# A hybrid Hyena/retention step: Hyena product in three pieces, residual chain rebuilt around adaLN work, two weight halves ahead in the opening

## The chip, the core and the metric

The kernel runs on one core of a Trainium2 chip. The metric is device time in microseconds (us) of one launch. The core has a matrix engine (TensorE, PE in the rows), three elementwise engines (VectorE = DVE, ScalarE = ACT, GpSimd = POOL), and SyncE (SP), which issues most of the transfers from memory. Each engine works through its own list of instructions in the order in which it was written; engines wait for one another through semaphores. A list that is held at its first instruction holds all that stands behind it.

## What is computed

One layer on two groups of 128 tokens of width 2048 (g = 0: context tokens, g = 1: latent tokens). Cut to what matters here:

```python
mod = silu(c) @ w_ada + b_ada              # 6 x 2048: shift, scale, gate for mixer and FFN (adaLN)
h   = rmsnorm(x, g_pre_m) * (1 + scale_m) + shift_m
proj = h @ w_in                            # Hyena v, x1, x2; retention q, k, v, g; two gates
z    = x1 * fftconv(v, kf[0], bias[0])     # convolution of 128 tokens by a Fourier product
y_hy = x2 * fftconv(z, kf[1], bias[1])
y_ret = retention(q, k, v, state) * silu(g)
merged = g_hy * (y_hy @ w_br_hy) + g_ret * (y_ret @ w_br_ret)
x = x + gate_m * rmsnorm(merged @ w_out, g_post_m)       # first residual
h2 = rmsnorm(x, g_pre_f) * (1 + scale_f) + shift_f
a, b = split(dwconv3(h2 @ ffn_w_up))
x = x + gate_f * rmsnorm((gelu(a) * b) @ ffn_w_down, g_post_f)
```

## The kernel before

**Products.** A weight matrix is read in *halves* of 256 x 512 numbers (512 KB). A half arrives as `raw`; ScalarE casts it to the upper part `wh` (L225) and VectorE subtracts to get the lower part `wl` (L226). The activations stand in two parts too (`hTh`, `hTl` and the like). TensorE then makes three products for each 128 rows and each group: wh with the upper part (L292), wl with the upper part (L293), wh with the lower part (L294); 12 matmuls for a half, 6 where the two groups are made apart.

**Order.** The program is written out by a planner, item by item (`run_items`). An item is the matmuls of one half or some adaLN matmuls (`ada`, L575). Behind each item `feed` writes splits until `st["L"]` halves are split ahead of their use, and transfers until `st["R"]` raws are outstanding; `depth(L, R)` sets both. `defer(us, f)` writes f once the planned matmul time has gone on by that many us, and small pieces of side work (`push`, `piece(cost, f)`) are written as a time budget allows; `drain` writes all that is left of them at once. What the planner wrote is the fixed order of each engine's list.

**Opening (about 25 to 285 us).** The adaLN vector for the mixer is made in six blocks (`mod_block`), each two or four columns of 128. For each: `ada` matmuls, a copy `adap` (L579), transposes `pcol` (L622), `colsum` and `colA` on VectorE, the affine step on `xnT`, then `hTh` on ScalarE (L678) and `hTl` on VectorE (L680). Eight projections over that block follow, with the next block's adaLN woven in. Halves of `w_in` are counted from 0 in this text; blocks after the first begin at halves 8, 16, 24, 32 and 48. Depth is `depth(3, 10)` (L719). Beside it runs the filter network of the convolution: `p` (L462), a sine chain `arg` on VectorE (L444 to L449), `h1T` on ScalarE (L450).

**Hyena (about 290 to 520 us).** As side work, `conv_fwd` (L794) makes two Fourier products `pu`, `pa`, six VectorE operations for the complex product `y` (L803 to L805), then `yh` and `yl` (L807, L808). The adaLN columns for the FFN (`ada_todo`, L709) run among the projections; their columns are turned (`to_cols`) 2.0 us of planned time after the last `ada` matmul.

**First residual (about 840 to 910 us).** `w_out` is multiplied in four column chunks. For the last ten halves (two of the third chunk, all eight of the fourth) the two groups stand apart, all of g = 0 before g = 1, so that the residual of g = 0 is made while TensorE does g = 1. `out_evac` takes squares (`jk`, L1271) and the gate product (`gm`, L1272); `chain_a` adds to x (`xr`, L1226) and squares (L1228); `chain_b` (L1232ff) ends in `diag` (L376), a diagonal matrix of 1/rms; `h2_block` turns 4 x 128 columns with it (`pt`, L1249), applies scale and shift (`h2v`, L1255, L1258) and splits (`h2Th` L1260, `h2Tl` L1261). The up-projection of the FFN begins with g = 0 of ten halves (`up_first`, L1388), counted 240 to 249 here, then their g = 1; `w_out`'s last chunk is 232 to 239.

Of the kernel before, what the change touches and what calls it, by code (L numbers as in the profile page):

```python
# [100 lines left out]
def hybrid_step(ctx: ExitStack, tc: tile.TileContext, ins, y_p, y_s, st_out):  # L101
# [692 lines left out]
    def conv_fwd(o, g, hf, src):  # L794
        def f():
            cs = slice(hf * W, hf * W + W)
# [43 lines left out]
    def hyena():  # L840
# [5 lines left out]
        F = lambda o, i: piece(4.8, conv_fwd(o, *gh[i], io[o][0]), True)  # L846
        I = lambda o, i: piece(0.6, conv_inv(o, *gh[i], io[o][1]), True)

        def fin(o):
            def f():  # L850
# [8 lines left out]
             load("x1", 1), S(0, 0), mul("x1", 0, 0), F(0, 0), S(0, 1), mul("x1", 0, 1), load("x2", 0), F(0, 1),  # L859
             I(0, 0), mul("x1", 1, 0), S(0, 2), mul("x1", 1, 1), load("x2", 1), F(0, 2), I(0, 1), S(0, 3),  # L860
             mul("x2", 0, 0), F(0, 3), I(0, 2), mul("x2", 0, 1), S(1, 0), mul("x2", 1, 0), I(0, 3), fin(0), F(1, 0),
             S(1, 1), mul("x2", 1, 1), F(1, 1), I(1, 0), S(1, 2), F(1, 2), I(1, 1), S(1, 3), F(1, 3), I(1, 2),
# [358 lines left out]
    def chain_a(g):  # L1221

        r = neg2_rstd(ssm[:, g, NBLK - 1:NBLK], mbase[g])
        ssx = small([P, 3], "ssx")
# [4 lines left out]
        xbase[g] = ssx

    def chain_b(g):
        ssx, b0, b1 = xbase.pop(g), small([P, 1], "b0"), small([P, 1], "b1")
        V.tensor_tensor(out=b0, in0=ssx[:, 0:1], in1=ssx[:, 1:2], op=ALU.add)
        V.tensor_scalar(out=b1, in0=b0, scalar1=1.0 / D, scalar2=RMS_EPS, op0=ALU.mult, op1=ALU.add)
        dg2[g] = diag_of(neg2_rstd(ssx[:, 2:3], b1))
        for h in range(2):
# [4 lines left out]

    def h2_block(g, j):
        def f():
# [3 lines left out]
            pt = aux((P, 4, P), "pt")  # L1247
            for kk in range(4):
                PE.matmul(pt[:, kk, :], lhsT=xr[g, j // 2][:, (j % 2) * W + kk * P:(j % 2) * W + (kk + 1) * P],  # L1249
                          rhs=dg2[g], start=True, stop=True)  # L1250
            val = s2("h2v").rearrange("p (a t) -> p a t", a=4)
            for kk in range(4):
                sc, sh = colA[:, 3, 4 * j + kk, g:g + 1], colA[:, 2, 4 * j + kk, g:g + 1]
# [259 lines left out]
```

## Time and profile before

| | us |
|---|---|
| median of three runs | 1639.85 (1639.69 to 1643.77) |
| the profiled execution | 1639.68 |
| its span in the trace | 1637.9 |
| TensorE busy | 1588.7, 97% of the span |
| TensorE weight loads busy | 1249.3, 76% |
| VectorE busy | 1191.9, 73% |
| ScalarE busy | 733.4, 45% |
| mean granted TensorE clock | 0.988 of full speed |

The span is 1.8 us shorter than the execution's time; what lies around it is nothing that the kernel orders. TensorE is idle 49 us in all, and more than half of that lies in the first 25 us and the last 10. So a change can take away only the few waits between, and the matmuls that run at half clock behind some of them; every wait that it adds shows in the time at once. The clock has two levels here, 1.0 (2.4 GHz) and 0.50 (1.2 GHz).

### The profile page before, as it was taken

To read this page: it belongs to the slowest core of one execution; us is meant where nothing else is said; L and a number is where in the kernel's file an instruction comes from. 1 tells how busy PE (TensorE), PEld (TensorE's weight loads), DVE (VectorE), ACT (ScalarE), POOL (GpSimd) and SP (SyncE) were. 2 spreads that over 40 slices of the span, in tenths; PEclk is the share of its full clock that TensorE was granted. 3 is DMA by queue.
4 is the path that set the end of the run, shared out by engine and by line. 5 is a ranking of instruction groups with operands and counts; after the bars stand their busy time and mean duration, and the time that the engine had idled before them with its cause. 6 is when DMAs were issued, how large, how long until landed. Compare 5 with 4: busy or idle time off the path is not lost.

```text
span 1637.9 us, 20339 instructions
## 1 busy us (share of the span) xinstructions
PE 1588.7 (97%) x7449; PEld 1249.3 (76%) x7449; DVE 1191.9 (73%) x1659; ACT 733.4 (45%) x946; POOL 69.0 (4%) x129
## 2 busy tenths in 40 slices
PE   5899999998999999999998999999999999999997
PEld 3566668776677887778887888888888888888886
DVE  2687866977775797678997655777778767778655
ACT  4523333243335346344545555455444355555532
POOL 0000012220001200000000000000000000000000
PEclk9899999999999999999999999999999999999999
DMA  9969898896676888898766765766678866766671
GB/s 331 336 187 326 280 311 267 259 343 201 206 245 220 296 267 298 306 335 279 266 201 219 227 173 179 215 200 200 211 249 266 298 184 190 216 206 203 207 239 52
DMA packets 208477, 396.88 MB, mean 242 GB/s; under 512 B 13221, under 2 KB 29920, under 8 KB 208377
## 3 DMA queue, kind: packets, MB, share of 16 engines
q1 hardware_dynamic: 201336, 373.88, 70.4%
q0 software_dynamic: 6800, 21.62, 4.2%
q8 instruction: 58, 0.95, 0.2%
q14 instruction: 43, 0.34, 0.1%
q10 hardware_dynamic: 240, 0.08, 0.0%
HBM read 384.03 MB, written 6.30 MB: 238 GB/s over the span
## 4 chain that ended last, share of the span: by engine, by line
PE 89%; DVE 4%; DMA 3%; issue 1%; SPq 1%; ACT 1%; DVEq 0%; ACTq 0%
PE acc L292 27%; PE acc L293 26%; PE acc L294 26%; PE ada L575 4%; DMA raw<-in_w_in_dram 2%; SPq L210 1%; PE put L1357 1%; DVE wl L226 1%; PE ph L484 1%; DMA raw<-in_ffn_w_up_dram 0%; ACT wh L225 0%; DMA vr<-in_norm_pre_mix_dram 0%; PE pt L403 0%; DVE h2v L1255 0%; PE pe L479 0%
## 5 line engine op out<-in xcount | busy, mean ns | idle before, releaser
L226 DVE TENSOR_TENSOR wl<-raw,wh 128x1024 fp32r<-128x1024 f32 x504 | 597.9, 1220 | 214.0 <-ACT wh L225 209.7
L225 ACT CAST wh<-raw 128x1024 fp32r<-128x1024 f32 x504 | 508.2, 1048 | 210.0 <-DMA raw<-in_w_in_dram 46.4
L292 PE MATMUL acc<-wh,hTh 128*128 128x512 f32 x704 | 285.0, 405 | 3.2 <-ACT wh L225 3.2
L292 PE MATMUL acc<-wh,h2Th 128*128 128x512 f32 x704 | 278.8, 396 | 1.7 <-ACT h2Th L1260 1.7
L293 PE MATMUL acc<-wl,hTh 128*128 128x512 f32 x704 | 277.4, 394 | 1.4 <-DVE wl L226 1.2
L294 PE MATMUL acc<-wh,hTl 128*128 128x512 f32 x704 | 276.6, 393 | 0.0
L294 PE MATMUL acc<-wh,h2Tl 128*128 128x512 f32 x704 | 275.3, 391 | 0.0
L293 PE MATMUL acc<-wl,h2Th 128*128 128x512 f32 x704 | 274.5, 390 | 0.0
L292 PEld LDWEIGHTS acc<-wh,hTh 128*128 128x128 f32 x704 | 133.7, 190 | 54.9 <-issue 19.5
L604 DVE SCALAR_TENSOR_TENSOR adac<-raw,cT,adac 128x512 f32<-128x512 f32 x240 | 164.6, 745 | 0.0
L293 PEld LDWEIGHTS acc<-wl,hTh 128*128 128x128 f32 x704 | 133.9, 190 | 29.7 <-DVE wl L226 3.0
L294 PEld LDWEIGHTS acc<-wh,hTl 128*128 128x128 f32 x704 | 133.6, 190 | 29.0
L294 PEld LDWEIGHTS acc<-wh,h2Tl 128*128 128x128 f32 x704 | 132.5, 188 | 28.8 <-DVE h2Tl L1261 0.4
L292 PEld LDWEIGHTS acc<-wh,h2Th 128*128 128x128 f32 x704 | 132.6, 188 | 28.4 <-ACT h2Th L1260 2.2
L293 PEld LDWEIGHTS acc<-wl,h2Th 128*128 128x128 f32 x704 | 132.8, 189 | 26.3
L292 PE MATMUL acc<-wh,actTh 128*128 128x512 f32 x352 | 137.3, 390 | 0.0
L294 PE MATMUL acc<-wh,actTl 128*128 128x512 f32 x352 | 137.1, 389 | 0.0
L293 PE MATMUL acc<-wl,actTh 128*128 128x512 f32 x352 | 137.0, 389 | 0.0
L1362 ACT ACTIVATE uv<-put,fcw 128x256 f32<-128x256 f32 x88 | 41.6, 474 | 86.4 <-DVE uv L1365 64.4
L1343 ACT COPY u<-acc 128x512 f32<-128x512 f32 x44 | 25.7, 587 | 119.7 <-PE acc L294 118.0
L294 PEld LDWEIGHTS acc<-wh,actTl 128*128 128x128 f32 x352 | 66.1, 188 | 13.9
L293 PEld LDWEIGHTS acc<-wl,actTh 128*128 128x128 f32 x352 | 66.1, 188 | 13.7
(311 smaller groups left out, 1595.9 us busy)
## 6 DMA issues: line engine op xcount, KB each, us to landing
raw<-in_w_ada_dram SPq DMA_DIRECT2D x192, 512.0 KB
raw<-in_w_in_dram SPq DMA_DIRECT2D x176, 512.0 KB
raw<-in_ffn_w_up_dram SPq DMA_DIRECT2D x176, 512.0 KB
raw<-in_ffn_w_down_dram SPq DMA_DIRECT2D x88, 512.0 KB
raw<-in_w_out_dram SPq DMA_DIRECT2D x32, 512.0 KB
raw<-in_w_br_hy_dram SPq DMA_DIRECT2D x16, 512.0 KB
raw<-in_w_br_ret_dram SPq DMA_DIRECT2D x16, 512.0 KB
shw<-in_hy_short_w_dram POOLq DMA_DIRECT2D x18, 256.0 KB, 8.3
```

The costliest lines, as they stand in the source:

```text
L210: SP.dma_start(out=h.raw.rearrange("p a n -> p (a n)").rearrange("p (a n) -> p a n", a=per), in_=h.src)
L225: A.copy(h.hi, h.raw)
L226: V.tensor_tensor(out=h.lo, in0=h.raw, in1=h.hi.bitcast(F32), op=ALU.subtract)
L292: PE.matmul(self.ps[g], lhsT=h, rhs=wh, start=first, stop=False)
L293: PE.matmul(self.ps[g], lhsT=h, rhs=wl, start=False, stop=False)
L294: PE.matmul(self.ps[g], lhsT=l, rhs=wh, start=False, stop=last)
L484: PE.matmul(ph, lhsT=h2fT, rhs=fl["w3", o, d][:, hf * W:hf * W + W], start=True, stop=True)
L575: PE.matmul(z["ps"][32 * t:32 * t + 32, :nt * P], lhsT=cT[:, kb + kk, 2 - 2 * i:34 - 2 * i], rhs=w[:, kk, :], start=i == 0 and kb + kk < 4 ...
L604: V.scalar_tensor_tensor(out=t, in0=w, scalar=c, in1=t if kt else bias, op0=ALU.mult, op1=ALU.add)
L1343: A.copy(u[:, g, :], ch.ps[g])
L1357: PE.transpose(pt[:, a, g, :], u[:, g, kk * P:(kk + 1) * P], ident)
L1362: A.activation(o, i, AF.Copy, scale=fcw[:, 1, col:col + 1])
```

## The change

It has three parts, and some bookkeeping.

**Opening.** `depth(3, 10)` becomes `depth(2, 8)` from the first block on until the projections behind the blocks: two halves split ahead instead of three, eight raws outstanding instead of ten.

**Hyena.** `conv_fwd` becomes three pieces of side work: the Fourier matmuls with the first half of the complex product, its second half, and the two parts. The FFN's adaLN columns are turned 8.0 us of planned time behind their matmuls instead of 2.0, and the last two columns of 128 are left for later. The gate row sums (`with_sums`) move from the `w_out` chunks to the projections.

**First residual.** The gate product is written into the gate's own tile, so `gm` goes; `xr` and its squares are made in four pieces of 512; `chain_b` follows `chain_a` at once; `h2_block` becomes `h2_turn` (transposes and two affine steps each on ScalarE and VectorE, in turn) and `h2_split`, written at staggered times; only the fourth chunk's halves are made group by group; the eight adaLN items left over stand as filler among g = 1 of the last chunk; the depth there is (3, 8) and grows later. A buffer more (`NS4`) is paid for by dropping the tile `ones`.

```diff
-    NS4, NS2 = 44, 8
+    NS4, NS2 = 45, 8
...
-    ones = cp.tile([P, P], F32, name="ones")
-    V.memset(ones, 1.0)
     onesr = cp.tile([P, P], F32R, name="onesr")
-    V.tensor_copy(onesr, ones)
+    ones = onesr.bitcast(F32)
+    ones0 = s2("ones0")[:, :P]
+    V.memset(ones0, 1.0)
+    V.tensor_copy(onesr, ones0)
...
-    ada_todo = deque(it for b in range(NBLK) for it in ada_units(SHIFT_F, 4 * b, 4, None))
+    turned = []
+    ada_todo = deque(it for t0, nt in ((0, 4), (4, 4), (8, 4), (12, 2)) for it in ada_units(SHIFT_F, t0, nt, None, 8.0))
...
-    its[7].post.append(depth(3, 10))
+    its[7].post.append(depth(2, 8))
...
-    def conv_fwd(o, g, hf, src):
+    def conv_fwd(o, g, hf):
+        def prod(i):
+            pu, pa, y, t = hyp["f", g, hf]
+            a, b, op = ((Kre, KB, ALU.subtract), (KB, Kre, ALU.add))[i]
+            V.tensor_tensor(out=y[:, i, :], in0=pu, in1=a[o][:, cs], op=ALU.mult)
+            V.tensor_tensor(out=t, in0=pa, in1=b[o][:, cs], op=ALU.mult)
+            V.tensor_tensor(out=y[:, i, :], in0=y[:, i, :], in1=t, op=op)
         def f():
             u = hyp.pop(("u", g, hf))
             pu, pa = aux(n="pu"), aux(n="pa")
             dft_mm(pu, "C", u[:, 0, :], u[:, 1, :])
             dft_mm(pa, "S", u[:, 0, :], u[:, 1, :])
-            y, t = s4([P, 2, W], n="y"), s2("yt")
-            for i, (a, b, op) in enumerate(((Kre, KB, ALU.subtract), (KB, Kre, ALU.add))):
...
+            hyp["f", g, hf] = pu, pa, s4([P, 2, W], n="y"), s2("yt")
+            prod(0)
+        def parts():
+            y = hyp.pop(("f", g, hf))[2]
             yh, yl = s4([P, 2, W], F32R, "yh"), s4([P, 2, W], F32R, "yl")
             A.copy(yh, y)
             V.tensor_tensor(out=yl, in0=y, in1=yh.bitcast(F32), op=ALU.subtract)
             hyp["y", g, hf] = (yh, yl)
-        return f
+        return piece(2.1, f, True), piece(2.1, lambda: prod(1)), piece(1.2, parts)
...
-        F = lambda o, i: piece(4.8, conv_fwd(o, *gh[i], io[o][0]), True)
+        F = lambda o, i: conv_fwd(o, *gh[i])
...
-            add(with_ada(with_sums(its, (1, 3, 2, 2)[j])))
+            add(with_ada(with_sums(its, (2, 3, 3, 3)[j])))
...
     def chain_a(g):
-        for n, (h, a, b) in enumerate(((0, 0, DH), (1, 0, W), (1, W, DH))):
-            V.scalar_tensor_tensor(out=xr[g, h][:, a:b], in0=gm[g, h][:, a:b], scalar=r, in1=xr[g, h][:, a:b],
-                                   op0=ALU.mult, op1=ALU.add)
-            A.activation(gm[g, h][:, a:b], xr[g, h][:, a:b], AF.Square, accum_out=ssx[:, n:n + 1])
+        for c in range(NBLK):
+            xs, m = xr[g, c // 2][:, (c % 2) * W:(c % 2) * W + W], gbc[GATE_M, c][:, g, :]
+            V.scalar_tensor_tensor(out=xs, in0=m, scalar=r, in1=xs, op0=ALU.mult, op1=ALU.add)
+            A.activation(m, xs, AF.Square, accum_out=ssx[:, c:c + 1])
...
-    def h2_block(g, j):
+    def h2_turn(g, j):
...
-            for kk in range(4):
+            for kk in (2, 0, 3, 1):
                 sc, sh = colA[:, 3, 4 * j + kk, g:g + 1], colA[:, 2, 4 * j + kk, g:g + 1]
-                if kk < 3:
+                if kk < 2:
...
+    def h2_split(g, j):
+        def f():
...
             A.copy(hg, val)
             V.tensor_tensor(out=lg_, in0=val, in1=hg.bitcast(F32), op=ALU.subtract)
...
-            if c % 2 == 0:
-                gm[g, h] = s4([P, DH], n="gm")
             A.activation(s2("jk"), ch.ps[g], AF.Square, accum_out=ssm[:, g, c:c + 1])
-            V.scalar_tensor_tensor(out=gm[g, h][:, cs], in0=ch.ps[g], scalar=-0.5, in1=gbc[GATE_M, c][:, g, :],
-                                   op0=ALU.mult, op1=ALU.mult)
+            m = gbc[GATE_M, c][:, g, :]
+            V.scalar_tensor_tensor(out=m, in0=ch.ps[g], scalar=-0.5, in1=m, op0=ALU.mult, op1=ALU.mult)
...
                 chain_a(g)
-                defer(0.1, lambda: chain_b(g))
-                for us, j in ((10.4, 0), (10.4, 1), (10.4, 2), (10.4, 3)):
-                    defer(us, h2_block(g, j))
+                chain_b(g)
+                defer(6.5, h2_turn(g, 0))
+                defer(7.8, h2_turn(g, 1))
+                defer(7.8, h2_split(g, 0))
+                for j in range(2, NBLK):
+                    defer(5.4 + 2.4 * j, h2_turn(g, j))
+                    defer(5.4 + 2.4 * j, h2_split(g, j - 1))
+                defer(15.0, h2_split(g, NBLK - 1))
...
             st["L"] += n
-            st["R"] += n
...
-        its = Chunk(act_m, KD, out_evac(c)).run(ins["w_out"][0], 0, c * W, 0, KD, (0, 0, 2, KD // 2)[c])
+        its = Chunk(act_m, KD, out_evac(c)).run(ins["w_out"][0], 0, c * W, 0, KD, KD // 2 if c == NBLK - 1 else 0)
...
-        add(with_sums(its, (3, 3, 3, 0)[c]))
+        add(its)
...
-            its[0].pre.append(depth(3, 2))
+        if c == 3:
+            its[0].pre.append(depth(3, 8))
...
-    grown = [it for i, it in enumerate(add(again)) if i >= 0][:5]
-    for it in grown:
+    fill = ada_units(SHIFT_F, 14, 2, lambda: turned.append(1), 1.2)
+    items.extend(again[:2] + fill[:4] + again[2:5] + fill[4:] + again[5:])
+    for it in again[6:]:
         it.post.append(grow(1))
...
-        first = add(a[:n] + b[:lead])
-        for it in first[:len(grown)]:
-            it.post.append(grow(-1))
+        first = a[:n] + b[:lead]
+        for i in range(4):
+            halves.extend(it.half for it in fill[2 * i:2 * i + 2] + first[i:i + 1])
+        halves.extend(it.half for it in first[4:])
+        items.extend(first)
+        for it in first[:3]:
+            it.post.append(grow(1))
```

Three places show what moves in the engines' lists. Numbers at the end of names only count tiles.

VectorE at the last block boundary of the opening. Before, the two `wl` ahead of the new block's `colsum` to `hTl` are halves 46 and 47, those behind it 48 and 49:

```order
L226 TENSOR_TENSOR wl_1931<-raw_1831,wh_1930 128x1024
L226 TENSOR_TENSOR wl_1961<-raw_1858,wh_1960 128x1024
L704 TENSOR_TENSOR q_582<-acc_466_1946,q_582 128x512
L704 TENSOR_TENSOR q_583<-acc_467_1947,q_583 128x512
L624 TENSOR_REDUCE colsum<-pcol_1980 128x16
L628 TENSOR_TENSOR colA<-colsum,bcol 128x4x2x2
L630 TENSOR_TENSOR colA<-colA,gpre 128x8
L641 TENSOR_SCALAR xnT_461<-xnT_461,colA 128x128 x4
L680 TENSOR_TENSOR hTl_1997<-xnT_461,hTh_1996 128x512 x2
L226 TENSOR_TENSOR wl_2003<-raw_1862,wh_2002 128x1024
L226 TENSOR_TENSOR wl_2023<-raw_1866,wh_2022 128x1024
```

With the change the two ahead are halves 45 and 46, those behind 47 and 48:

```order
L226 TENSOR_TENSOR wl_1921<-raw_1852,wh_1920 128x1024
L226 TENSOR_TENSOR wl_1951<-raw_1856,wh_1950 128x1024
L705 TENSOR_TENSOR q_572<-acc_462_1936,q_572 128x512
L705 TENSOR_TENSOR q_573<-acc_463_1937,q_573 128x512
L625 TENSOR_REDUCE colsum<-pcol_1970 128x16
L629 TENSOR_TENSOR colA<-colsum,bcol 128x4x2x2
L631 TENSOR_TENSOR colA<-colA,gpre 128x8
L642 TENSOR_SCALAR xnT_451<-xnT_451,colA 128x128 x4
L681 TENSOR_TENSOR hTl_1987<-xnT_451,hTh_1986 128x512 x2
L226 TENSOR_TENSOR wl_1993<-raw_1876,wh_1992 128x1024
L226 TENSOR_TENSOR wl_2013<-raw_1880,wh_2012 128x1024
```

Half 47, which the old block's products still use, has moved from in front of the new block's `hTl` to behind it.

ScalarE at the first Hyena product whose `yh` stood ahead of the adaLN copy `adap`. Before:

```order
L789 CAST us_3153<-v_307 128x512
L225 CAST wh_3168<-raw_3067 128x1024
L225 CAST wh_3191<-raw_3107 128x1024
L807 CAST yh_3221<-y_3213 128x1024
L579 COPY adap_3231<-ada_2534 128x512
L225 CAST wh_3255<-raw_3125 128x1024
L225 CAST wh_3273<-raw_3143 128x1024
```

With the change:

```order
L225 CAST wh_3157<-raw_3067 128x1024
L791 CAST us_3171<-v_303 128x512
L225 CAST wh_3186<-raw_3100 128x1024
L580 COPY adap_3211<-ada_2534 128x512
L225 CAST wh_3227<-raw_3121 128x1024
L225 CAST wh_3258<-raw_3139 128x1024
L707 ACTIVATE vr_3059<-acc_697_3082 128x512
L707 ACTIVATE vr_3060<-acc_698_3083 128x512
L225 CAST wh_3281<-raw_3161 128x1024
L225 CAST wh_3309<-raw_3190 128x1024
L818 CAST yh_3315<-y_3241 128x1024
L225 CAST wh_3331<-raw_3231 128x1024
```

The copy `adap` now stands seven instructions ahead of that `yh`, behind a weight cast.

VectorE behind the second residual chain (g = 1), from its `diag`. Before:

```order
L376 TENSOR_SCALAR diag_7288<-cst,nz_7282 128x128
L226 TENSOR_TENSOR wl_7323<-raw_7118,wh_7322 128x1024
L226 TENSOR_TENSOR wl_7333<-raw_7130,wh_7332 128x1024
L1255 TENSOR_SCALAR h2v_7349<-pt_7344,colA 128x128 x3
L1261 TENSOR_TENSOR h2Tl_7181<-h2v_7349,h2Th_7180 128x4x128
L1255 TENSOR_SCALAR h2v_7361<-pt_7356,colA 128x128 x3
L1261 TENSOR_TENSOR h2Tl_7195<-h2v_7361,h2Th_7194 128x4x128
L1255 TENSOR_SCALAR h2v_7373<-pt_7368,colA 128x128 x3
L1261 TENSOR_TENSOR h2Tl_7209<-h2v_7373,h2Th_7208 128x4x128
L1255 TENSOR_SCALAR h2v_7385<-pt_7380,colA 128x128 x3
```

With the change (the first `wl` is half 244, the one behind `h2Tl` half 245):

```order
L377 TENSOR_SCALAR diag_7283<-cst,nz_7277 128x128
L226 TENSOR_TENSOR wl_7288<-raw_7109,wh_7287 128x1024
L1285 TENSOR_TENSOR h2Tl_7302<-h2v_7228,h2Th_7301 128x4x128
L226 TENSOR_TENSOR wl_7306<-raw_7115,wh_7305 128x1024
L226 TENSOR_TENSOR wl_7310<-raw_7121,wh_7309 128x1024
L226 TENSOR_TENSOR wl_7324<-raw_7169,wh_7323 128x1024
L226 TENSOR_TENSOR wl_7328<-raw_7175,wh_7327 128x1024
L226 TENSOR_TENSOR wl_7342<-raw_7181,wh_7341 128x1024
L226 TENSOR_TENSOR wl_7346<-raw_7203,wh_7345 128x1024
L226 TENSOR_TENSOR wl_7360<-raw_7241,wh_7359 128x1024
L1269 TENSOR_SCALAR h2v_7376<-pt_7371,colA 128x128 x2
L226 TENSOR_TENSOR wl_7382<-raw_7291,wh_7381 128x1024
```

Half 244 is split behind the chain now instead of well before it, and seven more halves stand ahead of the first `h2v` of g = 1.

## Rows read from the trace of the kernel before

**Rows 1.** The view of waits, PE: us in total, times, longest.

```profile
PE pcol L622 <- ACT adap L579: 6.4, 2, 5.9
PE pt L1249 <- DVE diag L376: 2.6, 1, 2.6
PE p L462 <- ACT h1T L450: 2.3, 1, 2.3
PE pu L782 <- DVE us L790: 1.8, 1, 1.8
PE acc L292 <- ACT h2Th L1260: 1.7, 1, 1.7
PE pu L781 <- ACT us L789: 0.8, 1, 0.8
```

**Rows 2.** The view by windows; the last three numbers: granted clock, DMA share, GB/s.

```profile
45.00:48.40 3.40, 3.40 (x10) 2.62 (x8) 3.05 (x8) 0.11 (x1) 0.00 (x0) 0.50 1.08 364
393.40:396.60 3.20, 3.16 (x10) 2.68 (x11) 2.46 (x5) 0.93 (x1) 0.00 (x0) 0.50 0.13 49
451.20:454.60 3.40, 3.40 (x13) 0.99 (x12) 2.62 (x5) 0.00 (x0) 0.00 (x0) 0.50 0.75 231
877.90:881.30 3.40, 3.40 (x9) 2.62 (x9) 2.17 (x7) 1.07 (x2) 0.00 (x0) 0.50 0.92 339
892.60:896.00 3.40, 3.40 (x30) 3.40 (x31) 3.26 (x5) 1.38 (x3) 0.00 (x0) 1.00 0.11 45
```

**Rows 3.** Timeline near 39 us, DVE: start, duration, instruction, idle time before it.

```profile
39.62 1.23 DVE L226 TENSOR_TENSOR wl<-raw,wh 128x1024 fp32r<-128x1024 f32 x1 [4.36 <-ACT wh L225]
```

**Rows 4.** Timeline at the last block boundary, PE, ACT and DVE.

```profile
240.56 0.39 PE L292 MATMUL acc<-wh,hTh 128*128 128x512 f32 x1
243.28 0.39 PE L292 MATMUL acc<-wh,hTh 128*128 128x512 f32 x1
241.42 5.79 ACT L225 CAST wh<-raw 128x1024 fp32r<-128x1024 f32 x6
242.51 2.36 DVE L226 TENSOR_TENSOR wl<-raw,wh 128x1024 fp32r<-128x1024 f32 x2 [0.19 <-ACT wh L225]
```

**Rows 5.** Timeline at the four boundaries before it, PE and DVE in pairs.

```profile
64.30 0.39 PE L292 MATMUL acc<-wh,hTh 128*128 128x512 f32 x1
64.87 1.23 DVE L226 TENSOR_TENSOR wl<-raw,wh 128x1024 fp32r<-128x1024 f32 x1 [0.26 <-ACT wh L225]
109.91 0.49 PE L292 MATMUL acc<-wh,hTh 128*128 128x512 f32 x1
111.49 1.23 DVE L226 TENSOR_TENSOR wl<-raw,wh 128x1024 fp32r<-128x1024 f32 x1 [0.26 <-ACT wh L225]
140.62 0.39 PE L292 MATMUL acc<-wh,hTh 128*128 128x512 f32 x1
141.57 1.23 DVE L226 TENSOR_TENSOR wl<-raw,wh 128x1024 fp32r<-128x1024 f32 x1 [0.26 <-ACT wh L225]
184.01 0.79 PE L292 MATMUL acc<-wh,hTh 128*128 128x512 f32 x1
185.95 1.23 DVE L226 TENSOR_TENSOR wl<-raw,wh 128x1024 fp32r<-128x1024 f32 x1 [0.18 <-ACT wh L225]
```

**Rows 6.** Timeline at the first Hyena product, DVE and ACT.

```profile
391.08 0.69 DVE L805 TENSOR_TENSOR y<-y,yt 128x512 f32<-128x512 f32 x1
392.81 0.58 ACT L579 COPY adap<-ada 128x512 f32<-128x512 f32 x1
```

**Rows 7.** Timeline of the second residual chain, ACT and DVE.

```profile
885.46 0.59 ACT L1271 ACTIVATE jk<-acc 128x512 f32<-128x512 f32 x1
892.26 0.29 DVE L376 TENSOR_SCALAR diag<-cst,nz 128x128 f32<-128x128 f32 x1
892.54 2.36 DVE L226 TENSOR_TENSOR wl<-raw,wh 128x1024 fp32r<-128x1024 f32 x2
895.96 0.46 ACT L1258 ACTIVATE h2v<-pt,colA 128x128 f32<-128x128 f32 x1 [2.02 <-DVE h2v L1255]
```

More of the change, by code (lines that the diff above doesn't have):

```diff
@@ L792, in conv_split @@
         return f
[L794 removed]
+    def conv_fwd(o, g, hf):
+        cs = slice(hf * W, hf * W + W)
+        def prod(i):
[4 more added lines that the diff above has]
+            V.tensor_tensor(out=y[:, i, :], in0=y[:, i, :], in1=t, op=op)
         def f():
[L796 removed]
             u = hyp.pop(("u", g, hf))
@@ L858, in hyena @@
         push(piece(1.0, dft_split), mul("v", 0, 0), mul("v", 0, 1), load("x1", 0), mul("v", 1, 0), mul("v", 1, 1),
[L859 to L862, printed above, removed]
+             load("x1", 1), S(0, 0), mul("x1", 0, 0), *F(0, 0), S(0, 1), mul("x1", 0, 1), load("x2", 0), *F(0, 1),
+             I(0, 0), mul("x1", 1, 0), S(0, 2), mul("x1", 1, 1), load("x2", 1), *F(0, 2), I(0, 1), S(0, 3),
+             mul("x2", 0, 0), *F(0, 3), I(0, 2), mul("x2", 0, 1), S(1, 0), mul("x2", 1, 0), I(0, 3), fin(0), *F(1, 0),
+             S(1, 1), mul("x2", 1, 1), *F(1, 1), I(1, 0), S(1, 2), *F(1, 2), I(1, 1), S(1, 3), *F(1, 3), I(1, 2),
              piece(3.8, rope("q")), I(1, 3), fin(1))
@@ L883, in w_in_chunk @@
             its[-1].post.append(after)
-        return add(with_ada(its))
+        return add(with_ada(with_sums(its, 2) if c == 13 else its))
     dec_t = {}
@@ L1176, in branch @@
         its = Chunk(act_y(name), NH, br_evac(j, which)).run(ins["w_br_" + name][0], 0, j * W, 0, NH)
-        add(with_ada(with_sums(its, 1)) if which == 0 and j >= 2 else with_sums(its, 1))
+        add(with_sums(its, 1))
         its[0].pre.append(drain(lambda: (name, 1) in yT and yT[name, 1][2] == 2))
@@ L1246, in f @@
             hi, lo = h2T[j]
-            pt = aux((P, 4, P), "pt")
-            for kk in range(4):
[L1249 to L1253, printed above, removed]
-                if kk < 3:
-                    V.tensor_scalar(out=val[:, kk, :], in0=pt[:, kk, :], scalar1=sc, scalar2=sh, op0=ALU.mult,
-                                    op1=ALU.add)
-                else:
-                    A.activation(val[:, kk, :], pt[:, kk, :], AF.Identity, bias=sh, scale=sc)
+            val = h2v.pop((g, j))
             hg, lg_ = hi[:, :, g * P:(g + 1) * P], lo[:, :, g * P:(g + 1) * P]
@@ L1305, in hybrid_step @@
             its[0].pre.append(load_x)
-            its[0].pre.append(depth(3, 2))
-    grown = [it for i, it in enumerate(add(again)) if i >= 0][:5]
-    for it in grown:
+        if c == 3:
[3 more added lines that the diff above has]
+    for it in again[6:]:
         it.post.append(grow(1))
-    items[-1].post.append(lambda: mT.clear())
+    again[-1].post.append(lambda: mT.clear())
     fcw = cp.tile([P, 3, 88], F32, name="fcw")
```

33 lines of the change are left out of this document (21 added, 12 removed).

## The prediction

> **What bounds the kernel now.** I read the page's busy shares first: TensorE is busy 97% of the span, so the kernel is bound by a list of matmuls that the change does not shorten (the same adaLN items, moved). What can change is time in which TensorE waits, and time in which it runs at half clock. So the view of waits comes second [rows 1]: the reader is to see that the waits which this change can reach are few: 5.9 us at `pcol` behind `adap`, 2.6 at `pt` behind `diag`, 2.3 at `p` behind `h1T`, 1.8 and 0.8 at `pu`, 1.7 at `acc` behind `h2Th`; 15.1 us together. Third, the view by windows, for the granted clock [rows 2]: behind four of these places a stretch of 3.2 to 3.4 us ran at 0.50, and each costs half its length, since a matmul takes twice as long there. Last, the timeline at the places where the change takes something out of an engine's list or puts something in front of something else.
>
> **The change, part by part: opening.** The sine chain that ends in `h1T` stands on VectorE behind a `wl` that had waited 4.36 us for its `wh`, and that for its transfer [rows 3]. With two halves ahead that split stands behind the chain, so the chain starts some us sooner and the 2.3 us wait goes; the stretch at 45.0 to 48.4 us at 0.50 goes with it, 1.7 us. Gain: 2.3 + 1.7 = 4.0 us.
>
> The price is at the five places where a new block begins. There ScalarE and VectorE must make `hTh`, `hTl` from TensorE's own `pcol`, and the next splits stand behind them. Today the first split behind `hTl` is the new block's first half, which comes just in time: at the last boundary VectorE has two `wl` from 242.51 to 244.87, the first ready near 243.7, and TensorE starts half 48 at 243.28 [rows 4]. With the change the first split there is half 47, a whole half earlier in TensorE's list (the order rows of VectorE above). TensorE wants its `wh` at 240.56 and its `wl` one matmul later. A half of 12 matmuls takes 243.28 - 240.56 = 2.72 us, so a matmul 0.23. `wh` would be there near 242.5 (the cast at 241.42 is one of six in 5.79 us, about 1 us each), `wl` at 242.51 + 1.18 = 243.7. Since a wait for `wh` counts in the later one for `wl`, the stall is 243.7 - 240.8 = 2.9 us. Nothing of the chain in front (pcol to `hTl`) is shortened by the change, since it starts from TensorE; so nothing hides this.
>
> The other four go the same way, each with one pair of rows: the start of the old block's last half on TensorE, and the first `wl` behind `hTl` [rows 5]. Stall = `wl` start + 1.23 - (TensorE's start + 0.2 to 0.3): 64.87 + 1.23 - 64.53 = 1.6; 111.49 + 1.23 - 110.23 = 2.5; 141.57 + 1.23 - 140.85 = 2.0; 185.95 + 1.23 - 184.33 = 2.9. Sum of five: 11.9 us. At the first, `colsum` has one split less ahead of it, worth 0.3 at most; I leave it in the range.
>
> Then the clock. Waits of 2.3, 5.9, 1.8 with 0.8 just before, and 1.7 us were followed by a stretch at 0.50, one of 2.6 was not [rows 1, 2]. The five new ones come in two steps each (for `wh`, then for `wl`), 1.6 to 2.9 us. I take three of five falls, at 1.7 us: 5.1; bounds 0 and 8.5. Opening: -4.0 + 11.9 + 5.1 = **+13.0 us**.
>
> **Hyena.** `adap` leaves ScalarE at 392.81 + 0.58, behind a `yh` that needs the sixth operation of the product, ending at 391.08 + 0.69 [rows 6]; TensorE waits 5.9 us for it. With the change `adap` stands in front of `yh`, and `pcol` four halves behind its last matmul instead of one: the wait goes. The waits at `pu` (1.8 + 0.8) are for `us`, behind three splits that were themselves behind `yl`; with the product cut, fewer splits gather behind it, and I take them as gone. The half-clock stretches behind them, 3.2 and 3.4 us, give back 3.3. Gain: 5.9 + 2.6 + 3.3 = 11.8 us. A price: smaller pieces let side work fall behind, and what is left is written in one block before the first Hyena branch: twelve `pz` matmuls, six groups of transposes for q and k and four for y, with two rotary passes of six VectorE operations between them. One such operation of 128 x 512 takes about 0.6 to 0.7 us [rows 6], a pass near 4; TensorE's work between covers most of it. By hand I get 2.4 us of waits; bounds 0 and 6. Hyena: **-9.4 us**.
>
> **First residual.** Gone: 1.7 (`acc` behind `h2Th`), 2.6 (`pt` behind `diag`), and 1.7 of half clock at 877.9 to 881.3: -6.0. g = 0 has a clear run by hand, with the filler. For g = 1: today `jk` starts at 885.46 as soon as TensorE has closed the group, and `diag` is done at 892.55, 7.1 us [rows 7]. With the change `jk` stands on ScalarE behind the last `h2_turn` of g = 0 (its affine steps, 0.46 us each on ScalarE [rows 7], alternating with VectorE on one tile, some 1.8 us), a cast (0.6) and a weight cast (1.0), which begin with transposes 1.4 us ahead of the group's end: about 2.2 us later. Half 244 is split only behind `diag`, +1.2. TensorE has halves 240 to 243 to do, 4 x 1.36 = 5.4, and one matmul. Stall: 2.2 + 7.1 + 1.2 - 5.4 - 0.2 = 4.9 us (2.7 if `jk` were not held). Then seven `wl` of 1.18 stand ahead of g = 1's first `h2v` (order rows above), and two more per block of h2: VectorE needs about 4.9 us per block (two splits 2.4, an alternating turn 1.8, `h2Tl` 0.7), TensorE's two halves only 2.7. I get three waits near 1.9 by hand, 5.8; at best none, if ScalarE and VectorE overlap better. I take 4.0, nearer the upper end, since the order is fixed. One fall of the clock behind the 4.9: 1.7. Residual: -6.0 + 4.9 + 4.0 + 1.7 = **+4.6 us**.
>
> Dropping `ones`, the 45th buffer and the moved row sums cost nothing: they are on VectorE and ScalarE where these are not waited for.
>
> **Sum.** 13.0 - 9.4 + 4.6 = +8.2 us on the profiled 1639.68, which is 0.17 below the median of three: **1648 us**.
>
> **Rivals.** *The clock holds.* The new waits come in steps of about 1 to 2 us, and the one of 2.6 us before 892.6 was followed by 1.00 [rows 2]. Without any new fall: opening -4.0 + 11.9 = +7.9, Hyena -9.4, residual +2.9: +1.4, 1641 us. The Trainium skill, "TensorE: Matmul & The Clock Gate", section "HAM oscillation — how this bites in real kernels", says that only matmul gaps beyond a certain length bring the low clock back; by it none of the five would, while the rows of 45.0, 451.2 and 877.9 us show it behind waits that short. Chance 0.2.
>
> *The boundaries are half as dear, and the residual works as meant.* If the chain from `pcol` to `hTl` starts 1.2 us earlier, because one split less stands ahead of it on VectorE, the five stalls shrink by 1.2 each to 5.9, with no clock: opening +1.9; Hyena -9.4; residual -6.0 + 4.9 = -1.1: -8.6, 1631 us, faster. Against it: `colsum` waits for TensorE in four of five places, not for VectorE. Chance 0.13.
>
> *Everything new bites.* All five falls (+3.4 on the forecast's opening), a burst of 6 us before the Hyena branch (+3.6), 5.8 in h2 (+1.8): 1657 us. It decides where the side work is drained with nothing else for TensorE to do. Chance 0.12.
>
> **How the numbers follow.** The forecast, 1643 to 1654 us, has 0.55. Range: from 1637 (the clock holds, +1.4; the burst is empty, -2.4; half of the h2 waits, -2.0) to 1657; it leaves out most of the faster case and the tail of the last. 0.3% is 4.9 us, about what a measurement of this kernel can tell from no change. Of the forecast's chance 0.07 lies under 1644.8. So slower: 0.48 + 0.12 = 0.60; within: 0.07 + 0.20 = 0.27; faster: 0.13.
>
> **What would show it.** In the trace after: no wait at `p` near 40 us, and the matmuls behind it at full clock; five waits of `acc` L292/L293 for `wh` and `wl` before 250 us, 1.6 to 2.9 us each, with stretches at 0.50 behind some; no `pcol` wait near 390 us; `pt` no longer waiting for `diag`, but `acc` waiting near 885 us for a half's split. If the waits at the boundaries are under 1 us, the opening's term is wrong; if `acc` never waits between 885 and 910 us, the residual's is; if `pcol` still waits, the order of ScalarE was not what held it.

## The result and the profile after

| | before, us | changed, us |
|---|---|---|
| median | 1639.77 (four runs, 1639.37 to 1643.77) | 1654.82 (four runs, 1648.83 to 1655.44) |
| the profiled execution | 1639.68 | 1654.24 |
| its span | 1637.9 | 1652.4 |
| mean granted TensorE clock | 0.988 | 0.985 |

The changed kernel is slower: ratio 1.0076, 95% interval 1.0059 to 1.0093, which is 9.7 to 15.2 us; the medians stand 15.1 us apart.

First the page's first part of the changed kernel:

```profile
PE 1594.8 (97%) x7513; PEld 1257.1 (76%) x7513; DVE 1191.9 (72%) x1656; ACT 737.9 (45%) x959; POOL 72.5 (4%) x129
```

TensorE is busy 6 us more than before. Its work is the same (64 adaLN matmuls of 512 columns are made as 128 of 256, which is the whole difference in their number, and all adaLN matmuls together take 2 us less), so more of it ran at half clock; the other 8 us of the longer span are waits. The view of waits of the changed kernel, TensorE (us in total, times, longest), for [rows 1]:

```profile
PE acc L292 <- ACT wh L225: 11.6, 7, 3.4
PE acc L293 <- DVE wl L226: 5.9, 8, 0.8
PE acc L292 <- ACT h2Th L1284: 4.7, 2, 3.1
PE acc L292 <- DVE yTl L847: 3.2, 1, 3.2
PE pqt L988 <- DVE q L978: 2.6, 1, 2.6
PE pu L784 <- DVE us L792: 1.3, 2, 1.1
PE pcol L623 <- ACT adap L580: 0.5, 1, 0.5
```

Gone are `p` behind `h1T`, `pt` behind `diag`, and 5.9 of the 6.4 us of `pcol`. In their place stand waits for a weight's two parts (`wh`, 11.6, of which 3.2 is at the start of the kernel in both; `wl`, 5.9), for `h2Th` (4.7, where 1.7 was), and, as lines that were nowhere before, for `yTl` (3.2) and `q` (2.6). The half-clock stretches of the changed kernel behind these, by windows (the last three numbers are granted clock, DMA share, GB/s), for [rows 2]:

```profile
143.40:146.70 3.30, 3.30 (x10) 2.53 (x8) 2.22 (x3) 0.00 (x0) 0.00 (x0) 0.50 1.05 405
191.20:194.50 3.30, 3.30 (x9) 2.60 (x8) 1.97 (x4) 2.59 (x3) 0.00 (x0) 0.50 0.55 164
252.60:255.90 3.30, 3.30 (x10) 2.53 (x9) 0.85 (x2) 2.50 (x3) 1.03 (x2) 0.50 0.71 234
525.70:532.40 6.70, 6.14 (x17) 4.88 (x18) 1.70 (x3) 0.11 (x1) 0.00 (x0) 0.50 0.26 78
890.90:894.20 3.30, 3.01 (x9) 2.53 (x10) 3.30 (x5) 3.30 (x5) 0.52 (x1) 0.50 0.83 278
911.40:914.70 3.30, 3.30 (x8) 2.61 (x9) 1.57 (x2) 1.40 (x2) 0.00 (x0) 0.50 0.18 32
918.20:921.50 3.30, 3.30 (x9) 2.52 (x9) 0.03 (x1) 0.00 (x0) 0.07 (x1) 0.50 0.03 11
```

Seven stretches, some 27 us at 0.50, which cost half of that: three behind block boundaries, one behind the drained side work, three in the residual.

The last block boundary of the opening, for [rows 4], timeline of ScalarE, VectorE, TensorE (start, duration, instruction, idle time before):

```profile
249.32 5.78 ACT L225 CAST wh<-raw 128x1024 fp32r<-128x1024 f32 x6
250.40 2.36 DVE L226 TENSOR_TENSOR wl<-raw,wh 128x1024 fp32r<-128x1024 f32 x2 [0.17 <-ACT wh L225]
248.23 0.39 PE L294 MATMUL acc<-wh,hTl 128*128 128x512 f32 x1
250.41 0.50 PE L292 MATMUL acc<-wh,hTh 128*128 128x512 f32 x1 [1.80 <-ACT wh L225]
251.67 0.50 PE L293 MATMUL acc<-wl,hTh 128*128 128x512 f32 x1 [0.76 <-DVE wl L226]
252.01 0.40 PE L294 MATMUL acc<-wh,hTl 128*128 128x512 f32 x1
```

The first cast behind `hTh` starts at 249.32, the first `wl` behind `hTl` at 250.40, as the prediction's order said; TensorE waits 1.80 us for that `wh` and 0.76 for that `wl`. The other four boundaries read the same, with 0.41 + 0.77, 0.57 + 0.59 + 0.76, 0.80 + 0.76 and 1.39 + 0.77 us.

### The profile page after: what moved, and what is told of

Read it like the earlier page. It is cut to its first block, busy times and chain, and to the rows that moved or that the text cites. A ratio compares the mean times of both kernels' runs of the same rounds, so it can differ in the third digit from the quotient of the medians.

```text
span 1652.4 us, 20460 instructions
## 1 busy us (share of the span) xinstructions
PE 1594.8 (97%) x7513; PEld 1257.1 (76%) x7513; DVE 1191.9 (72%) x1656; ACT 737.9 (45%) x959; POOL 72.5 (4%) x129
## 4 chain that ended last, share of the span: by engine, by line
PE 85%; DVE 2%; ACT 1%; issue 0%; DMA 0%; DVEq 0%; ACTq 0%
PE acc L292 26%; PE acc L294 26%; PE acc L293 26%; PE ada L576 2%; PE put L1382 1%; DVE wl L226 1%; ACT wh L225 0%; PE pt L1262 0%; PE pg L662 0%; PE pg L661 0%; DMA raw<-in_w_in_dram 0%; PE pq L1056 0%; PE pr L1010 0%; PE pst L1032 0%; PE po L1046 0%
```

## The experiments

All ratios are against the kernel before, run on the same chip beside each kernel; its median there was 1640.2 (for `open_only`, `undo_open`, `cheap_pieces`, `res_depth4`), 1640.7 (`open_hybrid`, `hy_only`, `best`, `res_nogrow`) and 1639.9 us (`ahead2_raw10`, `hy_sums`, `final`, `final_h`). The ratios and the differences of medians do not always agree to the microsecond; a difference of 2 to 3 us between two kernels is not settled by them.

### The opening alone, and the rest without it

`open_only` is the kernel before with this edit, `undo_open` the changed kernel with its reverse:

```diff
-    its[7].post.append(depth(3, 10))
+    its[7].post.append(depth(2, 8))
```

> The kernel before with one number pair changed: depth(2, 8) instead of depth(3, 10) in the opening. Theory: the opening alone costs what the two traces show there. The wait at p (2.28 us) and the half-clock stretch behind it (1.7) go, five waits for a split at block boundaries come (1.2, 1.9, 1.6, 2.2, 2.6 us in the trace of the changed kernel, 9.4 in all), the wait of 0.7 at pi goes, and three falls of the clock cost 1.7 each: about +9, so 1647 to 1650 us. Rival: the boundary waits come from the other parts of the change (fewer buffers, other loads), and the opening alone keeps only its gain: 1635 to 1637 us.

Measured: 1654.8 us, ratio 1.0108 (1.0074 to 1.0142), +14.6 us by medians, more than was expected. Its waits:

```profile
PE acc L292 <- ACT wh L225: 8.1, 6, 3.2
PE acc L293 <- DVE wl L226: 5.3, 8, 0.8
PE pcol L622 <- ACT adap L579: 6.4, 2, 6.0
PE pt L1249 <- DVE diag L376: 2.8, 1, 2.8
```

The boundary waits are all there (4.9 us of `wh` beyond the 3.2 at the start, and five of 0.76 us of `wl`, 8.7 in all), while `pcol` and `pt` wait as before. The rival falls. The waits come near to what the theory said; the rest of the 14.6 is, by this profile, the clock and the slow steps behind each wait (worked out below for the last boundary): it has stretches at 0.50 behind four of the five boundaries, one more than the three counted on. One more, at 96.6 us, follows no wait; it is not the edit's, since it stands at the same matmuls in `hy_sums` and `final` too, which have the opening of the kernel before.

> The changed kernel with depth(3, 10) put back in the opening, all else as changed. Theory: the boundary waits go and the wait at p returns, about -9 us against the changed kernel, so 1643 to 1647 us; the waits near 520 us and between 885 and 920 us stay. Rival (the loss is in the Hyena and residual parts alone): no more than 3 us away from the changed kernel, 1651 to 1655 us.

Measured: 1637.0 us, ratio 0.9980 (0.9966 to 0.9994): a little faster than the kernel before, and 18 us below the changed one, twice what was expected. So on balance the change loses its time in the opening: the Hyena and residual parts together are worth -3.2 us, a sum of gains and losses that the next runs take apart.

### Which of the two numbers

> The kernel before with depth(2, 10): two halves split ahead, but ten raws outstanding as before. Theory: the boundary waits come from the split's place in the lists alone, so this is as slow as depth(2, 8) was: five waits of 1.2 to 2.6 us, 9 us in all, and several falls of the clock, 1651 to 1656 us. Rival: the eight raws are the cause (a weight that lands later); then the boundary waits are gone and the time is 1637 to 1641 us.

```diff
-    its[7].post.append(depth(3, 10))
+    its[7].post.append(depth(2, 10))
```

Measured: 1655.8 us, ratio 1.0088 (1.0064 to 1.0111), as with (2, 8). Its waits for `wh` and `wl` are like those of `open_only`:

```profile
PE acc L292 <- ACT wh L225: 8.3, 6, 3.2
PE acc L293 <- DVE wl L226: 6.7, 10, 0.8
```

Ten raws instead of eight bring nothing back; it is the place behind `hTl` of the half that is no longer split ahead that costs.

> The kernel before with depth(2, 8) only until the item of half 3, then depth(3, 10) as before. Theory: the sine chain keeps its place ahead of the third split, so the wait at p goes, and from half 4 on three halves are ahead again, so that no block boundary waits: -2 to -4 us against the kernel before, 1636 to 1638 us. Rival: two halves ahead in the first block already make the first boundary (half 7) late, or the loss of the depth is in the transfers; then 1640 to 1643 us.

```diff
-    its[7].post.append(depth(3, 10))
+    its[7].post.append(depth(2, 8))
...
+        if n == 0:
+            its[3].post.append(depth(3, 10))
```

Measured: 1639.0 us, ratio 0.9985 (0.9974 to 0.9996). No boundary waits and no wait at `p`, so the order works as meant; of the 4 us it should bring, 1.7 show by medians. Its trace, of the slowest of its ten runs, shows a new wait of 1.8 us for `wh` and 0.95 for `wl` at 330 us. It begins with a transfer: the cast at 322.16 had waited 6.95 us for its raw (3.82 in the kernel before, at 321.42), with a DMA share of 1.0 from 300 to 322 us in both, while TensorE was 2.4 us ahead (its `pu` at 314.14 instead of 316.54). At 332 us TensorE stands 0.7 us behind the kernel before, and a stretch at 0.50 follows from 332.9 us. So in that run (1643.97 us) the time saved was lost again at a transfer, as the second half of the rival has it; whether the other runs lose it there is not shown.

### Hyena: the pieces, and the row sums that came with them

`hy_only` is the kernel before with the three pieces and the later columns only; opening, residual and row sums as before.

```diff
-    ada_todo = deque(it for b in range(NBLK) for it in ada_units(SHIFT_F, 4 * b, 4, None))
+    ada_todo = deque(it for b in range(NBLK) for it in ada_units(SHIFT_F, 4 * b, 4, None, 8.0))
...
-        F = lambda o, i: piece(4.8, conv_fwd(o, *gh[i], io[o][0]), True)
+        F = lambda o, i: conv_fwd(o, *gh[i])
```

> The kernel before with the Hyena part alone: three pieces of 2.1, 2.1, 1.2 and the columns turned 8.0 us behind their matmuls; row sums, opening and residual as before. Theory: the wait at pcol (5.9 us), those near 378 and 450 us (0.8, 0.8, 1.8) and 3.3 us of half clock go, 12.6 us; with the row sums left in the w_out chunks the side work has time to be written, so that no block is drained ahead of the first Hyena branch and at most 1 to 2 us of new waits come: 1627 to 1630 us. Rival: the larger budget alone makes the block and its waits of 2.65 and 3.16 us near 510 us with a fall of the clock, as in the changed kernel: 1635 to 1638 us.

Measured: 1629.1 us, ratio 0.9917 (0.9896 to 0.9939): -11.6 us. Its waits between 290 and 560 us are none; `pcol` is left with 0.5 us, early in the opening (a wait of 1.6 us, `pt` behind `gt`, is new at 736 us). So this part is worth what its waits and their half clock came to, and the larger budget of the pieces leaves no block that TensorE would wait for. No run separates the three pieces from the later columns; which of the two took away the wait at `pcol` is not shown.

`hy_sums` adds to it the moved row sums:

```diff
-        return add(with_ada(its))
+        return add(with_ada(with_sums(its, 2) if c == 13 else its))
...
-            add(with_ada(with_sums(its, (1, 3, 2, 2)[j])))
+            add(with_ada(with_sums(its, (2, 3, 3, 3)[j])))
...
-        add(with_sums(its, (3, 3, 3, 0)[c]))
+        add(its)
```

> The kernel before with the Hyena part and, of the residual part, only the gate row sums moved: two to chunk 13, (2, 3, 3, 3) to the gates, none to w_out. Theory: each sum takes 2.4 us from the side work's budget, so the last inverse products and the q, k, y transposes are left over and written as one block ahead of the first Hyena branch; the waits of 2.65 (pqt for q) and about 3.2 us (acc for yTl) near 510 us come back, with a fall of the clock: +6 to +8 us against the Hyena part alone (1629.1), 1635 to 1637 us. Rival: the block comes from the last two adaLN columns being left out there or from the residual's tiles; then 1628 to 1631 us.

Measured: 1635.9 us, ratio 0.9973 (0.9956 to 0.9990): 6.8 us lost again. Its waits:

```profile
PE pqt L986 <- DVE q L976: 2.7, 1, 2.7
PE acc L292 <- DVE yTl L845: 1.8, 1, 1.8
PE pu L782 <- DVE us L790: 1.4, 2, 1.0
```

The waits of the changed kernel come back with the row sums, and two stretches at 0.50 with them, from 508.5 and 515.4 us. In the program each sum item takes 2.4 us from the budget by which side work is written; what is then left over is written in one block. The sums are work of VectorE too, four operations an item (`hy_sums`):

```profile
496.77 2.73 DVE L604 SCALAR_TENSOR_TENSOR adac<-raw,cT,adac 128x512 f32<-128x512 f32 x4
```

No run has the sums without their price in the budget, so the runs do not tell the one from the other. The block on VectorE, in the changed kernel (timeline):

```profile
515.91 0.68 DVE L831 TENSOR_TENSOR x<-pz,x 128x512 f32<-128x512 f32 x1
516.51 0.69 DVE L973 TENSOR_TENSOR ra<-q,cst 128x512 f32<-128x512 f32 x1
519.90 0.68 DVE L978 TENSOR_TENSOR q<-q,rb 128x512 f32<-128x512 f32 x1
520.50 0.68 DVE L831 TENSOR_TENSOR x<-pz,x 128x512 f32<-128x512 f32 x1
521.70 0.68 DVE L973 TENSOR_TENSOR ra<-k,cst 128x512 f32<-128x512 f32 x1
525.52 1.87 DVE L847 TENSOR_TENSOR yTl<-pyt,yTh 128x512 fp32r<-128x512 f32 x3
520.72 1.06 PE L988 MATMUL pqt<-cst,q 128*128 128x128 f32 x8 [2.65 <-DVE q L978]
526.26 0.80 PE L292 MATMUL acc<-wh,yTh 128*128 128x512 f32 x1 [3.16 <-DVE yTl L847]
```

From 515.91 to 527.4 VectorE works without a pause: a product with `pz`, six operations of the rotary pass of q (516.51 to 520.6), another product with `pz` and one `yTl`, six operations for k (521.70 to 525.6), and only then the other three `yTl`. TensorE's transposes of q wait 2.65 us for the first pass, and the first Hyena branch 3.16 us for the `yTl` behind the second.

> The changed kernel with the budgets of the three Hyena pieces at 1.9, 1.7 and 1.2 (4.8 as the one piece had before) instead of 2.1, 2.1 and 1.2. Theory: the side work is written earlier, so that the last inverse products (pz) no longer stand in the block drained ahead of the first Hyena branch; the waits of 2.65 us (pqt for q) and 3.16 us (acc for yTl) near 520 us and the 6.8 us at half clock behind them go or shrink below 1 us: -6 to -9 us, 1646 to 1649 us. Rival: the rotary passes on VectorE cause these waits wherever pz stands; then they stay, 1653 to 1655 us.

```diff
-        return piece(2.1, f, True), piece(2.1, lambda: prod(1)), piece(1.2, parts)
+        return piece(1.9, f, True), piece(1.7, lambda: prod(1)), piece(1.2, parts)
```

Measured: 1652.7 us, ratio 1.0079 (1.0059 to 1.0099), 2 us below the changed kernel by medians and no different by the ratio. Half of the theory held: the `pz` are out of the block and `pqt` no longer waits, but `yTl` still does, 3.3 us, since the pass of k stands ahead of it as before, and small waits of 0.2 to 0.8 us come near 342 us. The rival was right about that half. The half clock near 530 us is gone in this run's profile, yet its stretches at 0.50 behind 85 us come to 27 us in all, as in the changed kernel's: others stand at 96.9 and 110.5 us.

### The residual

> The changed kernel with depth(4, 8) instead of (3, 8) from the last chunk of w_out on. Half 244 is then split ahead of g = 1's residual chain instead of behind it. Theory: the chain of 9 to 10 us against four halves of cover (5.4 us) is the bound, and the late split only adds to it: TensorE does half 244, 1.4 us, then waits for diag instead, so the 4.2 us of wait near 886 us become about 3, and the h2Th waits near 908 and 916 us stay: -1 to -2 us, 1652 to 1654 us. Rival: the late split is the whole of that wait; then it goes, with its half-clock stretch: -5 to -6 us, 1648 to 1650 us.

```diff
-            its[0].pre.append(depth(3, 8))
+            its[0].pre.append(depth(4, 8))
```

Measured: 1660.9 us, ratio 1.0131 (1.0106 to 1.0156): 6 us slower than the changed kernel, which neither theory had. Its waits:

```profile
PE acc L292 <- ACT h2Th L1284: 10.4, 3, 3.7
PE pt L1262 <- DVE diag L377: 4.2, 2, 2.1
```

The late split is gone, and TensorE waits for `diag` in its place, 2.1 us in each group: the chain was the bound there, as the theory had it. But `h2Th` is waited for three times, 10.4 us, where the changed kernel had 4.7 in two. Behind the `diag` of g = 1 the same eight splits stand as in the changed kernel, and the first `h2v` comes at the same point (899.91 us, 899.60 there), while TensorE, with half 244 done, wants h2 sooner. Then come splits that themselves wait for TensorE:

```profile
906.97 1.23 DVE L226 TENSOR_TENSOR wl<-raw,wh 128x1024 fp32r<-128x1024 f32 x1 [1.92 <-PE acc L293]
915.74 1.04 ACT L225 CAST wh<-raw 128x1024 fp32r<-128x1024 f32 x1 [2.56 <-PE acc L293]
```

The steps of h2 stand behind them in the lists: `h2Th` is cast at 903.72, 912.57 and 920.90 us, in the changed kernel at 903.41, 909.84 and 916.30. That these splits wait for buffers which TensorE still reads is argued from the rows, no run tests it. So it is the splits written ahead, not too few of them, that hold the residual.

> The changed kernel with depth(3, 10) put back in the opening and without the three grow(1) on the first items of the up-projection: five splits instead of eight stand between g = 1's diag and its first h2v on VectorE. Theory: the waits for h2Th behind 895 us (3.32 and 2.36 us in the run that put back the opening alone) are that queue; three splits of 1.2 us less take the first away and most of the second, with a half-clock stretch, and the wait of 3.9 us near 877 us stays: -4 to -6 us against that run, 1631 to 1633 us. Rival: the alternating steps of h2v and not the splits set the pace; then the waits stay, 1636 to 1638 us.

```diff
-        for it in first[:3]:
-            it.post.append(grow(1))
```

(on the changed kernel with depth(3, 10) in the opening). Measured: 1630.8 us, ratio 0.9928 (0.9906 to 0.9950), 6.2 us below `undo_open`, slightly more than expected. VectorE behind the second chain's `diag` in the changed kernel, then in this one:

```profile
889.63 0.29 DVE L377 TENSOR_SCALAR diag<-cst,nz 128x128 f32<-128x128 f32 x1
889.91 1.23 DVE L226 TENSOR_TENSOR wl<-raw,wh 128x1024 fp32r<-128x1024 f32 x1
891.65 8.03 DVE L226 TENSOR_TENSOR wl<-raw,wh 128x1024 fp32r<-128x1024 f32 x7
899.60 0.41 DVE L1269 TENSOR_SCALAR h2v<-pt,colA 128x128 f32<-128x128 f32 x1
```

```profile
874.29 0.29 DVE L377 TENSOR_SCALAR diag<-cst,nz 128x128 f32<-128x128 f32 x1
874.58 1.23 DVE L226 TENSOR_TENSOR wl<-raw,wh 128x1024 fp32r<-128x1024 f32 x1
876.32 4.62 DVE L226 TENSOR_TENSOR wl<-raw,wh 128x1024 fp32r<-128x1024 f32 x4
880.86 0.40 DVE L1269 TENSOR_SCALAR h2v<-pt,colA 128x128 f32<-128x128 f32 x1
```

From `diag` to the first `h2v` it is 10.0 us with seven splits between (8.03 us) and 6.6 us with four (4.62). No wait for `h2Th` is left in this run, where `undo_open` had 5.7 us in two. The wait for the late `wh` stays: 3.42 us in both. Not all of the difference need be this edit's: `yTl`, in code that both share, was waited for 1.49 us here and 3.16 in the profile of `undo_open`.

### Putting together what gains

`best` is the kernel before with the opening of `open_hybrid` and Hyena pieces of 1.9, 1.7, 1.2 and the columns turned 8.0 us behind their matmuls, residual and sums as before. `final` is the changed kernel with depth(3, 10), those pieces and the edit of `res_nogrow`; `final_h` adds the opening of `open_hybrid` to it.

> A candidate that keeps what gains: the kernel before with two halves ahead only until half 3 (then three), three Hyena pieces of 1.9, 1.7 and 1.2, columns turned 8.0 us behind their matmuls; residual and row sums as before. Theory: the gains add, -2 to -4 in the opening and -9 to -12.6 in Hyena: 1624 to 1630 us. Rival: VectorE, busier per us of Hyena now, hands the waits on to us and yTl; then 1631 to 1637 us.

> The changed kernel with depth(3, 10) in the opening, Hyena pieces of 1.9, 1.7 and 1.2, and no grow(1) on the first items of the up-projection. Theory: the two repairs add; the wait of 2.65 us near 510 us goes, that for yTl (1.5 to 3.3) may stay; the wait of 3.4 + 0.5 us near 877 us stays: -2 to -4 us against 1630.8, 1627 to 1629 us. Rival: moved work hands the wait on elsewhere in Hyena, 1630 to 1632 us.

> As the run named final, and with two halves ahead in the opening until the item of half 3, then three. Theory: the wait at p and its half-clock stretch go too, as in the run that did this alone (-1 to -4 us against the same kernel without it): 1624 to 1628 us. Rival: what the opening saves is lost again in another fall of the clock; then no more than 1 us from the run named final.

Measured: `best` 1628.5 us (ratio 0.9917, 0.9893 to 0.9941), `final` 1630.4 (0.9943, 0.9923 to 0.9962), `final_h` 1630.3 (0.9933, 0.9911 to 0.9956). All three beat both kernels, by 9 to 12 us against the one before, and cannot be told from `hy_only` (1629.1) or `res_nogrow` (1630.8). `final`'s and `final_h`'s rivals were right: what the edits took away at one place was small, and `yTl` kept its 3.3 us. The simplest is `hy_only`: all the gain of this change that the runs can tell from none is in cutting the Hyena product and turning the columns later.

## Why the prediction was right or wrong

Forecast 1648 us and slower; measured 1654.8, or +12.5 us by the ratio against +8.2. That lies within its range of 1637 to 1657 us, and just above the band of 1643 to 1654 that it thought likeliest. The sign, and where the loss lies, were right; two terms were off and one sentence was wrong. It is not a sum in which errors cancel by luck: opening and Hyena both came out dearer than forecast, and the residual is open (below).

**Opening, +13.0.** Right. The single part costs 14.6 us by medians. The wait at `p` and its half clock went as said. The five waits came where the order put them, 9.4 us of idle time for 11.9 forecast. The difference is how idle time is read: behind each wait the next matmul takes 0.50 us of the row instead of 0.23 (251.67 - 250.41 = 1.26 = 0.50 + 0.76). Counted by starts, from the last matmul before the waits to the first behind them, the last boundary took 252.01 - 248.23 = 3.78 us for three spacings of 0.23: 3.1 lost, where the forecast had 2.9 and the waits show 2.56. Counted in this way the other four lose 1.7, 2.6, 2.1 and 2.7 us (1.6, 2.5, 2.0 and 2.9 forecast). The falls of the clock were three of five in the changed kernel's profile, as taken, and four in `open_only`'s.

**Hyena, -9.4.** The gain of 11.8 was right: `hy_only` shows 11.6 by medians (13.6 by the ratio). The price was mis-sized: 2.4 us, by hand, against waits of 2.65 + 3.16 and 1.28 left at `pu`, together 7.1, and 6.7 us at half clock, about 3. The waits of the block alone, 5.8, were within its stated bounds (0 to 6), but I took the lower half and gave it no fall of the clock; with the clock it is outside them. The step that failed is the sentence that the moved row sums cost nothing, since VectorE is not waited for there. They cost 6.8 us, by `hy_sums`: with them the rest of the side work falls behind, and TensorE waits for VectorE at the block that is left. Whether it is the 2.4 us that each takes from the budget or its 2.73 us on VectorE is not separated by a run. In the changed kernel the part is then worth about -12.6 + 7.1 + 3.1 = -2.4 by its trace, and 1629.1 to 1635.9 in the runs: -4 instead of -9.4.

**Residual, +4.6.** The mechanisms were right. The stall before half 244 was 3.42 + 0.76 us, 4.9 forecast; `jk` started late, behind the weight cast, and the chain took the time that it took before. Timeline of the changed kernel, for [rows 7]:

```profile
881.54 1.05 ACT L225 CAST wh<-raw 128x1024 fp32r<-128x1024 f32 x1
882.49 0.60 ACT L1290 ACTIVATE jk<-acc 128x512 f32<-128x512 f32 x1
889.93 0.50 PE L292 MATMUL acc<-wh,h2Th 128*128 128x512 f32 x1 [3.42 <-ACT wh L225]
891.19 0.80 PE L293 MATMUL acc<-wl,h2Th 128*128 128x512 f32 x1 [0.76 <-DVE wl L226]
```

The group's last matmul ends at 881.07, so `jk` is held for 1.4 us, where the prediction had 2.2 (its own terms, 1.8 + 0.6 + 1.0 - 1.4, give 2.0). From `jk` to the end of `diag` (its row stands with `res_nogrow`) it is 882.49 to 889.92, 7.4 us; 7.1 before. The waits for `h2Th` were two, 3.14 and 1.57, 4.7 for 4.0 forecast; that the splits ahead cause them is shown by `res_nogrow`, where they are gone with three splits fewer. Three falls of the clock stood there, not one. By the changed kernel's trace the part is worth about +8 (8.9 of waits and 5 of half clock for 6.0 before). Between runs it is less: `undo_open` stands 1.2 us above `hy_sums`, which lacks the rest of the residual part, with some 2 us of scatter on either side. How much of the residual's loss is real at the median is left open at +1 to +8.

**The rivals.** That the clock holds did not come about: seven stretches at 0.50 stand behind new waits. That section of the Trainium skill's page "TensorE: Matmul & The Clock Gate" ("HAM oscillation — how this bites in real kernels") has only long gaps bring the low clock; here it came behind waits of 0.80 + 0.76 us at 141 us. The faster rival needed boundary waits half as long; they were nearly whole. The last rival, everything biting, is nearest to the measured time: its burst of 6 us was 5.8, though the falls at the boundaries were three and not five.

**What is open.** The parts, each from a pair of runs, add to 14.6 - 11.6 + 6.8 + 1.2 = 11.0 us, the changed kernel stands at 12.5 by the ratio and 15.1 by medians. And by medians `undo_open` is 18 us below the changed kernel while the opening alone adds 14.6; by the ratios it is 15.7 and 17.7, the other way round, so the runs show no difference between the two. Where the clock falls differs from profile to profile, and each kernel has only one.

## What to carry to other kernels

Count a split-ahead depth against the longest stretch of other work that stands in the same list: here one half less put the next weight behind the new block's chain five times, at 1.2 to 2.6 us each, for a single wait of 2.3 us saved. Where a planner gives side work a budget, work that is moved is not free because its engine has time to spare over the whole span: at its new place it can make the other side work late, here for 6.8 us. And more splits written ahead are not always safer: behind the residual chain, three fewer took 6 us off, one more put 6 us on.

## What the hardware showed that was not expected

The same wait is not always followed by the low clock. `yTl` was waited for 3.30 us in three runs of nearly the same code; the 7 us behind it, by windows, in `cheap_pieces`, `final` and `final_h`:

```profile
528.00:535.00 7.00, 6.73 (x31) 5.57 (x32) 4.56 (x9) 1.94 (x2) 0.00 (x0) 1.00 0.52 150
```

```profile
511.00:518.00 7.00, 6.77 (x31) 5.57 (x32) 4.53 (x9) 1.90 (x2) 0.00 (x0) 1.00 0.52 152
```

```profile
510.00:517.00 7.00, 6.59 (x19) 5.23 (x20) 1.88 (x5) 1.02 (x2) 0.00 (x0) 0.55 0.27 76
```

The first two stayed at 1.00, the third was at 0.55 on average. The low clock also came without a wait: in `open_only` a stretch at 0.50 from 96.6 us, with TensorE busy throughout and no idle time before it, where the same place of the kernel before had 1.00:

```profile
92.00:96.60 4.60, 4.60 (x25) 1.52 (x25) 4.21 (x6) 1.17 (x3) 0.00 (x0) 1.00 0.73 227
96.60:100.00 3.40, 3.40 (x7) 2.00 (x6) 1.66 (x4) 1.33 (x2) 0.00 (x0) 0.50 0.21 39
```

In the 4.6 us ahead of it TensorE was busy, with 25 matmuls, most of them of less than full height or width in the timeline: `ada` with 128*32, `pe` with 8*128, `ph` with 65*128. Seven of the fourteen profiles have this stretch at the same matmuls, whatever their opening, and seven have not. With each stretch worth 1.7 us, one profile of a kernel cannot be compared with one of another to better than a few of them. The runs scatter too: the changed kernel's four lie 6.6 us apart, and those of the kernel before, thirteen or fourteen beside each set, 8 to 11; that more short waits mean more scatter is not shown.
